# Hybrid GLA/mLSTM decoder layer on one core: token blocks stored by pieces, another place for a weight sum, down sums and gate rows on other queues and stages

## The chip, the cores and the metric

The kernel runs on 1 core of one Trainium2 chip. The metric is the device time in microseconds; the kernel before has a median of 1929.68 us over 3 runs (1927.24 to 1930.09). A core has five instruction streams that each run in order: TensorE (PE; its weight loads are shown as PEld), VectorE (DVE), ScalarE (ACT), GpSimd (POOL) and SyncE (SP). SP, ACT and POOL issue DMAs, which 16 DMA engines carry out.

## The reference, cut

One decoder layer in float32 over 16 meta tokens and 1024 tokens (1040 positions, width 1024):

```
h = concat([meta, x])                                    # 1040 x 1024
proj = rms_norm(h, norm_mix) @ w_in + b_in
g_q, g_k, g_v, g_r, g_lr, m_q, m_k, m_v, m_o, m_i, m_f, gate_a, gate_b = split(proj)
o_gla = head_rms(gla_chunked(...)) * silu(g_r)           # 4 heads, 128 keys, 256 values
o_ml  = head_rms(mlstm_chunked(...)) * sigmoid(m_o)      # 4 heads
y = sigmoid(gate_a) * (o_gla @ w_branch_gla) + sigmoid(gate_b) * (o_ml @ w_branch_ml)
h = h + y @ w_out
u = causal_dwconv(rms_norm(h, norm_ffn) @ w_up); gate, up = split(u)   # 2 x 2816
h = h + (silu(gate) * up) @ w_down
return rms_norm(h, norm_final)[16:]
```

## The kernel before

Every float32 product is made of three products of rounded halves: an operand is split into a high part (ScalarE copies and rounds it) and a low part (VectorE subtracts). So each weight tile goes through a DMA into a raw tile, a ScalarE split and a VectorE split before TensorE can use it. TensorE is kept full; the other engines and the queues run beside it.

**Order.** The program is written in Python generators, and a scheduler lays the instructions of each engine out in one list, by priority (`hp(n)` raises it) and by when it reckons that an instruction is ready. On the chip each list runs strictly in order. `issue_after(x)` keeps an instruction from being placed ahead of `x`. Tiles of one tag share `bufs` buffers; a new tile waits until the old one's readers are done.

**Stages**, by the profile:

1. Norm of x into `xH`, `xL` (to about 60 us).
2. Heads (to about 642 us): four GLA heads (s = 0 to 3), then four mLSTM heads (4 to 7). The main line makes projections; `main()` calls `advance()` 1.15 times per projection group, and each call moves one step of the current head's side work (`gla`, `mlstm`, `small_rows`) and one step of the closing work of an earlier head (`post`). A `yield` is the border of a step. `decay(s + 1)` is computed inside `gla(s)`. What is left when the projections are used up is run by `while side or closing: advance()`.
   In `post` of heads 3 to 6, `token_sums(k)` makes on POOL four sums and differences of token blocks for the products of the gate stage and stores them to the DRAM tile `tsc`; and `half_load`/`half_sums` load a part of `ffn_w_down` (on POOL), make four differences on POOL and store them to `tdn` (a down sum; 22 of them over the kernel: three in the heads, seven in the gate stage, six beside the first branch product, six beside the second). The first three gate rows of gate_b are projected at the end of the heads through the tile tagged "gst", which has one buffer.
3. Gate stage (to about 945 us): the gates g_r, m_o, gate_a and the rest of gate_b, two columns blocks at a time (13 pairs), by a Strassen-like scheme of seven block products (V, X, Y, Z banks in `piece`; the evacuations are at lines 997 to 1013). It needs the token blocks T1 to T4, which `token_blocks` loads from `tsc` in two pieces of 258 and 256 columns and `token_splits` splits; and sums of weight blocks, made in `gate_weights`, which `place` puts into one of four places: three buffers of the tags "wH"/"wL", and one of "w4H"/"w4L". Two gate_b projections (`COVER`) run on TensorE while the blocks are loaded. After each pair from the ninth on, down sums are made.
4. Branch products: o_gla @ w_branch_gla (`bg`, j = 0 to 7), then o_ml @ w_branch_ml (`bm`). `load_o` loads the gated head outputs on POOL. `sb` is the gate_b row j: loaded, put through a sigmoid on ScalarE, multiplied by the product on VectorE (L1257), added to `yg` (L1258) and split into `yH`, `yL` for the next product. Rows alternate between two single buffers ("hn" and "gst"). The `yg` rows lie in the tags Y0 to Y7.
5. Output product with w_out (`po`), whose results are added to the rows of x (`hacc`, tile h1 in Y0, h2 in Y1 and so on).
6. FFN up (to about 1685 us) and down, which the change does not touch.

Of the kernel before, what the change touches and what calls it, by code (L numbers as in the profile page):

```python
# [9 lines left out]
F32 = mybir.dt.float32  # L10
# [35 lines left out]
def hybrid_kernel(ctx, tc, x, meta, norm_mix, w_in, b_in, gla_w_gate, gla_b_gate, gla_norm,  # L46
# [407 lines left out]
            st[:, t0:t0 + n], p, AF.Copy), bank)  # L454
        nc.scalar.dma_start(gsc["b"][j], st[:, :NP])

    tsc = dram.tile([4, 4, P, 514], F32, name="tsc")

    def token_sums(k):

        a, b = (hd.tile([P, T], F32, name=f"x{i}{k}", tag="r", bufs=2) for i in "ab")
        t = wp.tile([P, T], F32, name=f"tx{k}", tag="gst", bufs=1)
        for y, i in ((a, k), (b, k + 4)):
            nc.gpsimd.tensor_tensor(y[:, :NP], xH[:, i, T0:].bitcast(F32), xL[:, i, T0:].bitcast(F32), OP.add)
        first, second = slice(0, 514), slice(512, NP)
        t1, t2 = t[:, 0:514], t[:, 520:1034]
        for dst, x, y in ((t1, a[:, second], a[:, first]), (t2, b[:, second], t1),
                          (a[:, second], b[:, second], a[:, second]), (b[:, first], b[:, first], t2)):
            nc.gpsimd.tensor_tensor(dst, x, y, OP.subtract)
        for i, src in enumerate((t1, t2, a[:, second], b[:, first])):  # L470
            nc.sync.dma_start(tsc[i, k], src)


    NP2 = NJ // 2
# [87 lines left out]
    def post(s, o, om, sc, ncols):  # L562

        h = s % 4
        g = "g" if s < 4 else "m"
        for c in range(NC):
            nc.scalar.activation(o(c), o(c), AF.Copy, scale=sc[:, c + 1:c + 2])
        nc.scalar.activation(om, om, AF.Copy, scale=sc[:2, 0:1])
        for _ in range(3 if s != 3 else 5):
            yield  # L570
        for j in range(2):
            of = hd.tile([P, T], F32, name=f"of{s}_{j}", tag="r", bufs=2)
            for gi in range(2):
                tp = ps.tile([P, 4, P], F32, name=f"ot{s}_{j}_{gi}", tag="s", bufs=3)
                for i in range(4):
                    nc.tensor.transpose(tp[:, i, :], o(4 * gi + i)[:, j * P:(j + 1) * P], ident)
                a, b = 2 + 512 * gi, 2 + 512 * (gi + 1)
                nc.scalar.activation(of[:, a:b], tp.rearrange("p n w -> p (n w)"), AF.Copy, scale=ncols[j])
                if gi == 0:
                    yield  # L580
            tp = ps.tile([P, 4, P], F32, name=f"otm{s}_{j}", tag="s", bufs=3)
            nc.tensor.transpose(tp[:, 0, :2], om[:, j * P:(j + 1) * P], ident[:2, :2])
            nc.vector.tensor_scalar(of[:, 0:2], tp[:, 0, :2], ncols[j], None, OP.mult)
            nc.sync.dma_start(osc[g][2 * h + j], of[:, :NP])
            yield
        if 3 <= s < 7:
            token_sums(s - 3)
            if s < 6:
                for _ in range(2):
                    yield  # L590
                t = half_load(wp, "gst")
                for _ in range(3):
                    yield
                half_sums(*t)
# [24 lines left out]
    def gla(s):  # L619
# [144 lines left out]

        if s < 3:
            decay(s + 1)
        up = ps.tile([P, 2, DV], F32, name=f"u0{s}", tag="s", bufs=3)
        nc.tensor.matmul(up[:, 0, :], K0, vt[:NM, 0, :DV], start=True, stop=True)
        S = state(f"S{s}")
# [259 lines left out]
    def gate_weights(q):  # L1029
# [9 lines left out]
        def place(name):  # L1039
            nonlocal ngw  # L1040
            ngw += 1
            if ngw % 4 == 0:
                return [gs.tile([P, NK, P], F32R, name=f"g{p}{name}_{q}", tag="w4" + p) for p in "HL"]
            return [wp.tile([P, NK, P], F32R, name=f"g{p}{name}_{q}", tag="w" + p) for p in "HL"]

# [34 lines left out]
    def token_blocks():  # L1080
        for i in (0, 2, 1, 3):
            if i == 1:
                places()
            TB[i] = [gs.tile([P, 4, 514], F32R, name=f"T{p}{i}", tag=f"T{p}{i}") for p in "HL"]
        for c in (slice(0, W0), slice(W0, 514)):
            for i in (0, 2, 1, 3):
                nc.sync.dma_start(TB[i][1][:, :, c].bitcast(F32), tsc[i].rearrange("k p c -> p k c")[:, :, c])

    def token_splits(p):
        c = (slice(0, W0), slice(W0, 514))[p]  # L1090
# [46 lines left out]
    for q in range(NG):  # L1137
# [18 lines left out]
            next(g)  # L1156
            behind_ = g
        if q >= NK:
            for _ in range(2 if q < NK + 2 else 1):
                half_sums(*half_load(gs, "o0"))  # L1160
    next(behind_)
    for j in END:
# [58 lines left out]
    for j in range(NK):  # L1221
# [7 lines left out]
        if j == 1:  # L1229
            with tc.issue_after(opened.ins), tc.issue_after(loaded.ins):  # L1230
                om_, loaded = load_o("m", r1b, "R", nc.gpsimd)
        for i in ((), (), (5, 6, 7), (6, 7), (7,), (), (), ())[j]:
            half_sums(*half_load(r2, f"Y{i}"))

    yH = [r2.tile([P, NK, 2, 256], F32R, name=f"yH{i}", tag=f"OH{i}") for i in range(2)]
# [6 lines left out]
        return t[:, 2:NP].rearrange("p (h q w) -> p h q w", h=2, q=2)[:, :, i, :]  # L1242

    for j in range(NK):
        if j % 2:
            sb = r2.tile([P, T], F32, name=f"sb{j}", tag="hn", bufs=1)[:, :NP]
        else:
            sb = wp.tile([P, T], F32, name=f"sb{j}", tag="gst", bufs=1)[:, :NP]
        with tc.issue_after(loaded.ins):
            nc.gpsimd.dma_start(sb, gsc["b"][j])  # L1250
        with tc.issue_after(opened.ins):
            nc.scalar.activation(sb, sb, AF.Sigmoid, bias=cc(C_GB + j))
        pt = prod3(ubm[j], om_, j < 1, f"bm{j}")
# [10 lines left out]
                nc.scalar.activation(yh, z, AF.Copy)  # L1264
                nc.vector.tensor_tensor(yL[i][:, j], z, yh.bitcast(F32), OP.subtract)
        if half:
            half_sums(*half_load(r2, f"Y{j if j < 3 else 3 - j % 2}"))
    r1b_ctx.close()
    ps2_ctx.close()
    psF = ctx.enter_context(tc.tile_pool(name="psF", bufs=1, space=PSUM, reuse_waits="tile"))  # L1270
# [7 lines left out]
    for t in range(NC + 1):  # L1278
# [1 line left out]
        if t == 0:  # L1280
            nc.sync.dma_start(a[:2, :D], meta[T0:NM, :])
        else:
            (nc.gpsimd if t in (3, 4, 7, 8) else nc.sync).dma_start(a[:, :D], x[P * (t - 1):P * t, :])
        hacc.append(a)
    gffn = wp.tile([P, T], F32, name="gffn", tag="gst", bufs=1)[:, :D]
    nc.sync.dma_start(gffn, rowb(norm_ffn, 0, D))
# [542 lines left out]
```

## Time and profile before

| | |
|---|---|
| runs | 1927.24, 1929.68, 1930.09 us |
| profiled execution | 1930.77 us, its span 1928.9 us |
| mean granted TensorE clock | 0.987 |
| TensorE busy | 1872.7 us |
| VectorE, ScalarE, GpSimd busy | 1196.0, 854.5, 399.6 us |
| DMA | 270.02 MB, mean 140 GB/s |

Times are us from the start of the span. In a list of instructions the columns are start, duration (from the first to the last, where several are merged), engine, line, operation, tiles (out<-in), forms and count; the bracket at the end holds how long the engine stood idle before it and what ended that. A row of a list of waits reads: engine and line that waited, on which engine's instruction, total us, times, longest. A row of windows gives for a stretch the busy time of each engine, the granted clock (PEclk, 1.00 is full speed), the share of the DMA engines' time and the rate. A queue row (q0: POOL's DMAs, q1: SP's, q10: ScalarE's) gives packets, MB and share.

### The profile page before, as it was taken

What the parts mean: (1) busy time and instruction counts of PE and PEld (TensorE: products, weight loads), DVE (VectorE), ACT (ScalarE), POOL (GpSimd) and SP (SyncE); (2) the same over time, 40 slices, a digit from 0 to 9 for tenths busy, and PEclk for the clock granted to TensorE, in tenths of its full rate; (3) what the DMA queues carried; (4) which work ended last, traced back from release to release, by engine and by line L of the source; (5) the groups of instructions that cost most, each with busy time, mean ns of one, the idle gap of its engine ahead of it and who ended that gap; (6) DMA issues with size and microseconds to landing.
All of it is one profiled execution on the core that took longest, in us unless ns stands there. A gap on an engine that the chain in (4) does not pass through costs nothing. (4 is left out here: it accounts for less than half of the span.)

```text
span 1928.9 us, 32657 instructions
## 1 busy us (share of the span) xinstructions
PE 1872.7 (97%) x13377; PEld 1789.9 (93%) x13377; DVE 1196.0 (62%) x1775; ACT 854.5 (44%) x1369; POOL 399.6 (21%) x441
## 2 busy tenths in 40 slices
PE   8999999989999999999899989999999999999998
PEld 8899989989998899999899989999999999987776
DVE  6556646564652456665442335788878788786777
ACT  5354555535553433332432224544344343455573
POOL 3101101130442001125461520012222222200000
PEclk8999999999999999999999989999999999999999
DMA  5111021051433737675973653423333333288794
GB/s 166 34 36 58 15 66 50 21 156 58 121 88 99 197 97 163 158 171 168 299 267 107 197 169 114 138 77 110 117 116 109 110 110 119 91 295 321 274 377 161
DMA packets 222592, 270.02 MB, mean 140 GB/s; under 512 B 13486, under 2 KB 176832, under 8 KB 222443
## 3 DMA queue, kind: packets, MB, share of 16 engines
q1 hardware_dynamic: 201467, 198.89, 33.8%
q0 software_dynamic: 16832, 58.80, 9.5%
q10 hardware_dynamic: 4144, 10.26, 1.5%
q8 instruction: 105, 1.72, 0.4%
q14 instruction: 44, 0.36, 0.1%
HBM read 198.33 MB, written 69.57 MB: 139 GB/s over the span
## 5 line engine op out<-in xcount | busy, mean ns | idle before, releaser
L489 POOL TENSOR_TENSOR ts<-ts 128x256 f32<-128x256 f32 x88 | 77.4, 884 | 64.9 <-DMA ts<-in_ffn_w_down_dram 62.6
L1389 POOL TENSOR_TENSOR SB<-SA,rg 128x512 f32<-128x512 f32 x20 | 32.1, 1607 | 236.0 <-issue 114.1
L1476 PE MATMUL po<-wH_wo,yH 128*128 128x256 f32 x256 | 74.2, 290 | 5.8 <-ACT wH_wo L106 4.9
L201 PE MATMUL pv<-wH_gv,xH 128*128 128x256 f32 x256 | 75.3, 294 | 0.0
L201 PE MATMUL pv<-wH_mv,xH 128*128 128x256 f32 x256 | 74.7, 292 | 0.1
L1476 PE MATMUL po<-wL_wo,yH 128*128 128x256 f32 x256 | 73.2, 287 | 0.9 <-DVE wL_wo L107 0.9
L1476 PE MATMUL po<-wH_wo,yL 128*128 128x256 f32 x256 | 72.9, 286 | 0.0
L201 PE MATMUL pv<-wH_gv,xL 128*128 128x256 f32 x256 | 72.0, 281 | 0.0
L201 PE MATMUL pv<-wL_gv,xH 128*128 128x256 f32 x256 | 72.0, 281 | 0.0
L201 PE MATMUL pv<-wL_mv,xH 128*128 128x256 f32 x256 | 72.0, 281 | 0.0
L201 PE MATMUL pv<-wH_mv,xL 128*128 128x256 f32 x256 | 71.9, 281 | 0.0
L1203 PE MATMUL bg<-ogH,wH_bg 128*128 128x342 f32 x192 | 62.3, 325 | 3.9 <-ACT ogH L1186 3.9
L1424 DVE SCALAR_TENSOR_TENSOR cv<-u,fc,cv 128x1024 f32<-128x1024 f32 x44 | 65.3, 1484 | 0.4
L699 POOL TENSOR_TENSOR pk<-pk,kT 128x256 f32<-128x256 f32 (+1 forms) x24 | 29.6, 1233 | 163.6 <-ACT pk L697 163.6
L1371 POOL TENSOR_TENSOR A<-u2raw,A 128x512 fp32r<-128x512 f32 x20 | 43.9, 2196 | 92.8 <-ACT A L1370 92.8
L1203 PE MATMUL bg<-ogL,wH_bg 128*128 128x342 f32 x192 | 62.1, 325 | 0.6 <-DVE ogL L1187 0.6
L1203 PE MATMUL bg<-ogH,wL_bg 128*128 128x342 f32 x192 | 61.9, 323 | 0.0
L1203 PE MATMUL bm<-omH,wH_bm 128*128 128x342 f32 x192 | 61.4, 320 | 0.0
L1203 PE MATMUL bm<-omH,wL_bm 128*128 128x342 f32 x192 | 61.3, 319 | 0.0
L1203 PE MATMUL bm<-omL,wH_bm 128*128 128x342 f32 x192 | 61.2, 319 | 0.0
L1476 PEld LDWEIGHTS po<-wH_wo,yH 128*128 128x128 f32 x256 | 49.3, 193 | 7.1 <-ACT wH_wo L106 5.1
L1713 POOL TENSOR_TENSOR fr<-fv,mhalf 128x1 f32<-128x1 f32 x8 | 6.4, 805 | 229.6 <-DVE fv L1711 229.6
(752 smaller groups left out, 7480.4 us busy)
## 6 DMA issues: line engine op xcount, KB each, us to landing
gw<-in_w_in_dram SPq DMA_DIRECT2D x26, 512.0 KB
ts<-in_ffn_w_down_dram POOLq DMA_DIRECT2D x44, 256.0 KB, 4.5
tdn<-ts POOLq DMA_DIRECT2D x44, 256.0 KB, 2.9
rg<-in_ffn_w_up_dram SPq DMA_DIRECT2D x22, 512.0 KB
ru<-in_ffn_w_up_dram SPq DMA_DIRECT2D x22, 512.0 KB
adr<-s SPq DMA_DIRECT2D x40, 256.0 KB
rd<-in_ffn_w_down_dram SPq DMA_DIRECT2D x20, 512.0 KB
do<-tdn SPq DMA_DIRECT2D x18, 512.0 KB
```

What stands on the lines that cost most here:

```text
L201: nc.tensor.matmul(pt[:, :DV], a[:, k, t0:t0 + P], b[:, k % 4, :], start=(i == 0), stop=(i == 3 * NK - 1))
L489: nc.gpsimd.tensor_tensor(t[:, o], t[:, a], t[:, b], OP.subtract)
L699: eng.tensor_tensor(e, e, k, OP.mult)
L1203: nc.tensor.matmul(pt[:, i, :n], a[:, k, :], b[k][:, t0:t0 + n], start=(k == 0 and j == 0), stop=(k == NK - 1 and j == 2))
L1371: eng.tensor_tensor(l, src, h.bitcast(F32), OP.subtract)
L1389: late.tensor_tensor(sb[:, 0:4], sa[:, 0:4], rg[:, 0:4], OP.subtract)
L1424: nc.vector.scalar_tensor_tensor(y, u[:, j:SEQ + j], fc[:, j, jj:jj + 1], y, OP.mult, OP.add)
L1476: nc.tensor.matmul(pt[:, :DV], a, b[:, k % 4, :], start=(k == 0 and i == 0), stop=(k == NK - 1 and i == len(terms) - 1))
L1713: nc.gpsimd.tensor_tensor(rs, v, mhalf, OP.pow)
```

## The change

- The token blocks are kept in DRAM as two tensors, one per piece, with a partition's four blocks of a piece side by side; `token_sums` stores each source in two pieces, from POOL instead of SP (32 stores instead of 16), and works in a tile of the tag "of" (two buffers) instead of "gst". `half_load` in `post` is kept behind the last of these stores.
- `post` of head 3 has six instead of five yields ahead of its transposes, and four more ahead of `token_sums`. `gla` has a yield after `decay`.
- `place` uses the fourth place for the third, seventh and so on instead of the fourth, eighth and so on.
- One down sum moves from after the last gate pair to j = 4 of the first branch product. The six beside the second branch product use Y0 and Y1 in turn.
- The gate_b rows of the second branch are loaded by SP instead of POOL and without the wait for the head outputs' loads; rows 6 and 7 lie in Y2 and Y3.
- Of the rows of x, tiles 1 and 2 are loaded by POOL and the others by SP; before, it was tiles 3, 4, 7 and 8 by POOL.

```diff
-    tsc = dram.tile([4, 4, P, 514], F32, name="tsc")
+    tsc = [dram.tile([4, P, 4, n], F32, name=f"tsc{n}") for n in (258, 256)]
...
-        t = wp.tile([P, T], F32, name=f"tx{k}", tag="gst", bufs=1)
+        t = hd.tile([P, T], F32, name=f"tx{k}", tag="of", bufs=2)
...
         for i, src in enumerate((t1, t2, a[:, second], b[:, first])):
-            nc.sync.dma_start(tsc[i, k], src)
+            for p in range(2):
+                stored = nc.gpsimd.dma_start(tsc[p][i, :, k], src[:, 258 * p:258 * p + 258 - 2 * p])
+        return stored
...
-        for _ in range(3 if s != 3 else 5):
+        for _ in range(3 if s != 3 else 6):
             yield
...
         if 3 <= s < 7:
-            token_sums(s - 3)
+            for _ in range(4 if s == 3 else 0):
+                yield
+            stored = token_sums(s - 3)
             if s < 6:
                 for _ in range(2):
                     yield
-                t = half_load(wp, "gst")
+                with tc.issue_after(stored.ins):
+                    t = half_load(wp, "gst")
...
         if s < 3:
             decay(s + 1)
+            yield
...
-            if ngw % 4 == 0:
+            if ngw % 4 == 3:
                 return [gs.tile([P, NK, P], F32R, name=f"g{p}{name}_{q}", tag="w4" + p) for p in "HL"]
...
-        for c in (slice(0, W0), slice(W0, 514)):
+        for p, c in enumerate((slice(0, W0), slice(W0, 514))):
             for i in (0, 2, 1, 3):
-                nc.sync.dma_start(TB[i][1][:, :, c].bitcast(F32), tsc[i].rearrange("k p c -> p k c")[:, :, c])
+                nc.sync.dma_start(TB[i][1][:, :, c].bitcast(F32), tsc[p][i])
...
         if q >= NK:
-            for _ in range(2 if q < NK + 2 else 1):
+            for _ in range((2, 2, 1, 1, 0)[q - NK]):
                 half_sums(*half_load(gs, "o0"))
...
-        for i in ((), (), (5, 6, 7), (6, 7), (7,), (), (), ())[j]:
+        for i in ((), (), (5, 6, 7), (6, 7), (6, 7), (), (), ())[j]:
             half_sums(*half_load(r2, f"Y{i}"))
...
-        if j % 2:
-            sb = r2.tile([P, T], F32, name=f"sb{j}", tag="hn", bufs=1)[:, :NP]
+        if j % 2 or j > 5:
+            sb = r2.tile([P, T], F32, name=f"sb{j}", tag="hn" if j < 6 else f"Y{j - 4}", bufs=1)[:, :NP]
         else:
             sb = wp.tile([P, T], F32, name=f"sb{j}", tag="gst", bufs=1)[:, :NP]
-        with tc.issue_after(loaded.ins):
-            nc.gpsimd.dma_start(sb, gsc["b"][j])
+        nc.sync.dma_start(sb, gsc["b"][j])
...
-            half_sums(*half_load(r2, f"Y{j if j < 3 else 3 - j % 2}"))
+            half_sums(*half_load(r2, f"Y{j % 2}"))
...
-            (nc.gpsimd if t in (3, 4, 7, 8) else nc.sync).dma_start(a[:, :D], x[P * (t - 1):P * t, :])
+            (nc.gpsimd if t in (1, 2) else nc.sync).dma_start(a[:, :D], x[P * (t - 1):P * t, :])
```

## The prediction

> **What bounds the kernel now.** I read the page's engine totals first, then TensorE's own list of waits, then the stretches around each wait, and last the instruction order of the other engines there.
>
> ```profile
> PE 1872.7 (97%) x13377; PEld 1789.9 (93%) x13377; DVE 1196.0 (62%) x1775; ACT 854.5 (44%) x1369; POOL 399.6 (21%) x441
> engine line waited for: us in total, times, longest us
> PE Xg L978 <- DVE gu L998: 5.7, 1, 5.7
> PE po L1476 <- ACT wH_wo L106: 4.9, 1, 4.9
> PE bg L1203 <- ACT ogH L1186: 3.9, 1, 3.9
> PE pv L188 <- ACT qT L438: 3.2, 1, 3.2
> PE op L911 <- DVE dn L914: 2.6, 2, 2.1
> PE ot L576 <- ACT of L578: 2.1, 1, 2.1
> PE u L768 <- DVE la L613: 2.1, 2, 1.0
> PE po L1476 <- DVE wL_wo L107: 0.9, 2, 0.7
> PE bg L1203 <- DVE ogL L1187: 0.6, 2, 0.3
> PE po L1476 <- ACT yH L1264: 0.5, 1, 0.5
> PE po L1476 <- DVE sb L1257: 0.4, 1, 0.4
> ```
>
> TensorE is busy 97% of the span, 1872.7 of 1928.9 us, and the change removes no matmul. It can only gain from the 56 us in which TensorE stands still, and from the lower clock that follows a stop:
>
> ```profile
> core 0: us, PE busy (x) PEld busy (x) DVE busy (x) ACT busy (x) POOL busy (x), PEclk, DMA share, GB/s
> 600.00:605.00 5.00, 3.81 (x11) 3.09 (x12) 1.77 (x6) 3.13 (x12) 0.00 (x0) 0.70 0.85 262
> 676.00:680.00 4.00, 3.73 (x17) 3.73 (x18) 0.54 (x2) 0.39 (x1) 0.00 (x0) 0.50 0.48 125
> 940.00:950.00 10.00, 5.79 (x34) 5.07 (x32) 2.55 (x3) 5.16 (x7) 4.28 (x9) 0.84 1.03 351
> 950.00:960.00 10.00, 9.77 (x50) 9.49 (x51) 6.58 (x6) 5.40 (x6) 3.21 (x7) 0.82 1.03 348
> 1140.00:1146.00 6.00, 4.46 (x16) 3.65 (x17) 4.99 (x8) 2.54 (x5) 0.53 (x1) 0.50 0.46 139
> 1146.00:1150.00 4.00, 4.00 (x28) 4.00 (x27) 3.30 (x8) 1.36 (x3) 0.53 (x1) 0.74 0.65 209
> ```
>
> The granted clock (PEclk) is 0.50 to 0.84 in these rows, which hold or follow the long waits. Busy time by (1 - clock) is what a stop costs on top: 3.81 x 0.30 = 1.1 us at 600; 3.73 x 0.50 = 1.9 at 676; 0.9 + 1.8 = 2.7 at 940 to 960; 2.2 + 1.0 = 3.2 at 1140 to 1150. Each part of the change touches one of these places.
>
> **Heads: the token sums and the yields.**
>
> ```profile
> 400.73 0.35 DVE L839 SCALAR_TENSOR_TENSOR wt<-MB,tcol,big 128x128 f32<-128x128 f32 x1
> 401.45 3.02 POOL L464 TENSOR_TENSOR xa<-xH,xL 128x1026 f32<-128x1026 f32 x1 [11.74 <-DMA oscg<-of]
> 404.62 8.11 DVE L839 SCALAR_TENSOR_TENSOR wt<-MB,tcol,big 128x128 f32<-128x128 f32 x6
> 412.81 1.28 ACT L841 ACT_TABLE_LOAD   x1 [11.50 <-DVE wt L839]
> 424.68 0.70 POOL L491 DMA_DIRECT2D tdn<-ts  x1
> 582.63 2.39 POOL L464 TENSOR_TENSOR xa<-xH,xL 128x1026 f32<-128x1026 f32 x1 [14.33 <-DMA oscm<-of]
> 599.84 0.46 ACT L453 ACTIVATE gb<-pj 128x342 f32<-128x342 f32 x1 [8.21 <-DMA tsc<-tx]
> 635.82 1.04 PE L576 MATMUL ot<-ident,or 128*128 128x128 f32 x8
> ```
>
> The first token sums start on POOL at 401.45, and one VectorE operation of L839 goes from 0.35 us to 8.11 / 6 = 1.35. ScalarE, in order, sits 11.50 us for their result, with TensorE's evacuations of qT queued behind it: that is the 3.2 us wait of L188. The change starts these sums one plus four yields later. A head has 15 projection groups, which at the pace of 1.15 make 17.25 steps; the first sums start at 401.45 and the fourth at 582.63, 60.4 us a head, so a step is 3.5 us and they start near 419, when L839 is done. They then slow other VectorE work; the smaller of the two L911 waits, 2.6 - 2.1 = 0.5 us, is the nearest price. I take -2.7 us (bounds -3.2 and 0).
>
> At 599.84 ScalarE has stood 8.21 us for the store of tx, because tx shares the one buffer "gst" with the row being evacuated; TensorE lost 2.1 us and 1.1 us of clock. In "of" there is no such sharing: -3.2 us (bounds -3.2, 0). The yield after decay puts projection matmuls between the pre-activation banks and the u product that waits 1.0 us for each of two: -2.1 (bounds -2.1, and 0 if the wait moves along). The sixth yield of head 3 lets its transposes come one group later than the 2.1 us wait of L576: half of it, -1.0 (bounds -2.1, 0).
>
> The 16 stores on SP become 32 on POOL. An issue there takes 0.70 us, so a head pays 5.6 us of an engine that is busy 21%; behind them stand the down load, its sums and the next head's root. On the path: 0 now; what it costs if POOL runs out is a rival below. SP loses 16 issues that waited for POOL in front of weight loads, also 0, since no weight wait of the heads is in the list. One cost: the side work was 68 yields of four GLA heads + 11 + 52 of four mLSTM heads + 7 of the last closing = 138, and the main loop gives 120 x 1.15 = 138 steps. Three more decay yields make 141, so the end of the last closing has no projection between it. Its 8 transposes took 1.04 us: +1 us (bounds 0 and 3 x 3.5 = 10). Heads together: -8.0 us.
>
> **Gate start: the token blocks by pieces and the third place.**
>
> ```profile
> 643.89 12.45 SPq L1087 DMA_DIRECT2D TL<-tsc  x8
> 668.02 1.06 ACT L1093 ACTIVATE TH<-TL 128x1024 fp32r<-128x1024 f32 x1 [3.26 <-DMA TL<-tsc]
> 672.52 0.39 ACT L997 ACTIVATE gu<-Vg 128x258 f32<-128x258 f32 x1 [0.40 <-ACT gb L453]
> 644.00:652.00 8.00, 8.00 (x53) 8.00 (x52) 2.66 (x4) 0.46 (x1) 0.00 (x0) 1.00 0.97 201
> q1 hardware_dynamic: 526, 0.92, 56.7%
> q0 software_dynamic: 513, 1.86, 98.5%
> ```
>
> Eight loads of some 0.52 MB (4.2 MB) take SP 12.45 us to issue and land until 668. ScalarE has the last split ahead of the first evacuation, which comes only at 672.52; X waits for it: the 5.7 us. The q1 row is 644 to 652: 0.92 MB in 526 packets, 1.7 KB each, with all queues at 201 GB/s. The q0 row is 945 to 950, the gate outputs in rows of 4.1 KB: 1.86 MB in 5 us, 372 GB/s. After the change a partition's block lies in one piece of 4128 or 4096 bytes, a quarter of the descriptors. At 372 GB/s the blocks are in by 644 + 11.3 = 656; at 201 GB/s by 665, still 3 us sooner, about the 3.26 us for which the last split waits. I take the first, since the row length is that of the q0 row. The third sum of pair 0 goes to the fourth place, free from the start, so its split need not wait for the cover products; what it displaces in later pairs is hidden, as the list has no other wait of the gate's own products. Gain 5.7 + 1.9 = 7.6 us (bounds 2 and 7.6).
>
> The Trainium skill (DMA: Bandwidth & Descriptors, "Why small descriptors are slow (HBM only)") speaks against this size: it puts the loss at about three cycles per packet beside its 32-byte beats, by my estimate 9% at 1032 bytes. By that the blocks come 1.6 us sooner, this term would be 2 instead of 7.6, and the time 1909; the 201 against 372 GB/s rows go beyond it, though other traffic is in both.
>
> **Gate end: six down sums.**
>
> ```profile
> 938.27 0.69 POOL L491 DMA_DIRECT2D tdn<-ts  x1 [0.30 <-POOL ts L489]
> 939.50 2.67 POOL L1185 DMA_DIRECT2D ogL<-otdg  x5
> ```
>
> POOL finishes the seventh sum at 938.27 and only then issues the loads that TensorE waits for. Without it POOL is free sooner by the course of one down sum, and 1 MB of traffic goes. The loads then wait for the gate's own tiles to come free. Stake 3.9 + 0.6 + 2.7 = 7.2 us. Against it: rows 0 and 1 of the second branch gate lose their wait on the loads and may go in here on SP, 1.05 MB at 351 GB/s, 3 us. I take -5 (bounds -7.2, 0). The sum itself moves to the first branch product, where TensorE has no row that waits for POOL: 0.
>
> **Second branch: gate rows on SyncE.**
>
> ```profile
> 1096.56 1.29 DVE L1265 TENSOR_TENSOR yL<-sb,yH 128x512 fp32r<-128x512 f32 x2 [0.36 <-ACT yH L1264]
> 1109.73 0.57 POOL L1250 DMA_DIRECT2D sb<-gscb  x1
> 1138.25 1.15 ACT L1252 ACTIVATE sb<-sb,col 128x1026 f32<-128x1026 f32 x1 [6.46 <-DMA sb<-gscb]
> 1139.31 1.04 ACT L106 ACTIVATE wH_wo<-wr_wo 128x1024 fp32r<-128x1024 f32 x1
> ```
>
> Row 5's buffer is free at 1097.8 but POOL issues its load at 1109.73, behind the down sums: 12 us lost. Rows 6 and 7 inherit it through the two buffers, and ScalarE's last sigmoid at 1138.25 stands ahead of the split of the first output weights. On SP row 5 goes at once, and rows 6 and 7 have own places (Y2, Y3) because the late sums keep to Y0 and Y1. A row on SP waits for the splits of the row two before; the weight load behind it is made two products ahead. Stake 4.9 + 0.7 + 0.5 + 0.4 + 3.2 = 9.7; I take -9 (bounds -9.7 and -4, a later row still in the way). The x rows swap queues; they are only added after the first output products: 0.
>
> **Sum.** -8.0 - 7.6 - 5 - 9 = -29.6. A list laid anew makes small waits; six of the present size of 0.5 us are +3. That is -26.6. The profiled execution took 1930.77 us (span 1928.9 and 1.87 around it), 1.09 over the median; off the median 1929.68 it leaves 1903.
>
> **Rivals.** (1) Half: SP becomes the crowded queue. Rows 0 and 1 delay the first branch's loads, rows 2 to 5 hold up weights behind them, and the heads trade waits. For: SP waits in nearly every stage. Against: no SP load's own lateness heads the list above. Gate start 5, branch edges 4 + 4, heads 2: 15, so 1915.
> (2) Slower: POOL cannot issue. Place: heads 3 to 6. A head has 60 us; sums and down sums take POOL from 401.45 to about 426, 25 us, and 8 stores come to them. From (60 - 25) / 8 = 4.4 us per store POOL sets the pace, and from 5.1 us it outweighs the 22 us gained elsewhere; at 6 us a head is 13 us longer, four heads 52, less 22: 1960. Against it: the row at 424.68 shows 0.70 us. For it: the L839 rows show that POOL and VectorE slow each other.
> That is also a rule of the Trainium skill (SBUF — State Buffer, "SBUF: two separate sides"): certain VectorE operations lock GpSimd out of a port it needs to write descriptors. The 0.70 us here is the issue with VectorE partly busy, so it has a small chance.
> (3) Nothing: every wait comes back one instruction later, since ScalarE and VectorE stay in order; 1928 to 1931.
>
> **How the numbers follow.** Forecast 0.60, its own range 1894 (all stakes: 35 us) to 1911; half 0.23, 1911 to 1925; slower 0.12; nothing 0.05. Within 0.2% (3.9 us) is what this measurement cannot tell from no change. Faster 0.83, same 0.05, slower 0.12. The range runs from 1894 to 1928 and leaves out mostly the slower case.
>
> **What would show it.** Right: no wait of X for gu over 1 us, the block splits done before the cover products end; the first bg product on the heels of the last gate product; no wait for wH_wo; no ScalarE wait for the tsc stores. Wrong: POOL issues over 2 us in the heads, SP waits for yL ahead of weight loads, or new TensorE waits above 3 us with a clock of 0.5 behind them.

## The result and the profile after

| | kernel before | changed kernel |
|---|---|---|
| device time, median (range), us | 1929.68 (1927.24 to 1931.8), 7 runs | 1923.57 (1917.53 to 1925.63), 7 runs |
| profiled execution, its span, us | 1930.77, 1928.9 | 1925.63, 1923.6 |

The ratio is 0.9964, 95% interval 0.9951 to 0.9976: faster by 6.1 us where 26.6 were forecast. Run once more in the experiments, beside the kernel before on one chip, the changed kernel took 1921.18 us to 1932.79, a ratio of 0.9936 (0.9923 to 0.9949). The gain is 6 to 12 us.

TensorE's list of waits in the changed kernel answers to the one shown of before; the rows left out are short, or as long as before (columns: microseconds in all, times, the longest):

```profile
PE Xg L984 <- DVE gu L1004: 9.2, 2, 8.1
PE bg L1209 <- ACT ogH L1192: 3.9, 1, 3.9
PE op L917 <- DVE om L902: 3.8, 2, 2.8
PE pdV L1630 <- DVE db L1610: 3.4, 2, 2.9
PE u L774 <- DVE la L618: 2.8, 3, 1.1
PE Yg L984 <- DVE gu L1012: 1.1, 1, 1.1
PE pe L158 <- ACT gu L1011: 1.0, 1, 1.0
PE ot L578 <- ACT of L580: 0.9, 1, 0.9
```

The waits for qT (3.2), for dn (2.6, now 0.8) and for wH_wo (4.9) are gone or small. The wait at the gate start has grown from 5.7 to 8.1, the one before the first branch product stands at 3.9 as before, and the waits for om are new.

Where the time went is read from the start of the same instruction in TensorE's timelines, in microseconds of the span; "again" is the second profile of the changed kernel, "all" the last experiment:

| first instruction of | before | changed | difference | again | all |
|---|---|---|---|---|---|
| cover product pc (end of the heads) | 641.95 | 639.13 | -2.8 | 638.67 | 632.35 |
| first S2 product, Xg<-TH,gHSB | 676.27 | 676.63 | +0.4 | 675.74 | 660.79 |
| first S4 product, Yg<-xH,gHSB | 685.35 | 685.18 | -0.2 | 685.70 | 667.89 |
| first branch product bg | 948.70 | 951.87 | +3.2 | 949.79 | 929.73 |
| second branch product bm | 1042.67 | 1045.06 | +2.4 | 1043.42 | 1023.17 |
| up product Vu | 1250.31 | 1242.35 | -8.0 | 1240.65 | 1220.42 |
| down product pdV | 1702.09 | 1693.74 | -8.4 | 1693.45 | 1672.36 |
| end of the span | 1928.9 | 1923.6 | -5.3 | 1919.7 | 1900.5 |

The gain is made between bm and Vu: 10.4 us, in both profiles of the changed kernel. The heads bring 3, and all or nearly all of it is lost before the first S2 product (+0.4 and -0.5 there). What differs between the two profiles of the changed kernel is no part of the change: the start-up (the first value product at 72.64 and 70.69, 71.31 before), the wait for db (3.4 and 1.2) and the small waits for gu at L1011 and L1012 (2.1 and 0.8), 5.5 us together. The two measured gains differ by as much, but half of that is the kernel before, which took 3.1 us longer on the second chip. Nor is a row of the table good to a microsecond: the run of the branch part alone, below, has the heads and the start of the gate stage unchanged, and there the first S2 product came at 677.96 after a wait of 7.2 us and bg at 952.52, where the column of before has 676.27, 5.7 and 948.70.

At the gate start VectorE's timeline shows what the S2 product waits for (columns: start, duration, instruction, and in brackets the idle time ahead of it and what ended it):

```profile
668.57 2.37 DVE L1100 TENSOR_TENSOR TL<-TL,TH 128x1024 fp32r<-128x1024 f32 x2 [4.09 <-ACT TH L1099]
672.23 0.69 DVE L1060 TENSOR_TENSOR gS<-gw,gw 128x512 f32<-128x512 f32 x1 [1.29 <-DMA gw<-in_w_in_dram]
672.96 0.69 DVE L1061 TENSOR_TENSOR gw<-gw 128x512 f32<-128x512 f32 x1
673.57 1.22 DVE L1043 TENSOR_TENSOR gLA<-gw,gHA 128x1024 fp32r<-128x1024 f32 x1
674.82 0.69 DVE L1066 TENSOR_TENSOR gw<-gw,gw 128x512 f32<-128x512 f32 x1
675.54 0.69 DVE L1067 TENSOR_TENSOR gw<-gw 128x512 f32<-128x512 f32 x1
676.15 0.42 DVE L1004 TENSOR_TENSOR gu<-Xg,gu 128x258 f32<-128x258 f32 x1
```

The add at 676.15 frees bank X. Five operations on the weights of the *next* pair stand ahead of it on VectorE's list, and the first of them waits for the load of those weights (gw), which SP issues behind the token blocks. Nothing of the present product is late. In the kernel before, ScalarE's split of the same weights and, from VectorE's list, the first and the last row behind it:

```profile
669.77 1.06 ACT L1036 ACTIVATE gHA<-gw 128x1024 fp32r<-128x1024 f32 x1 [0.35 <-DMA gw<-in_w_in_dram]
```

```profile
670.87 1.22 DVE L1037 TENSOR_TENSOR gLA<-gw,gHA 128x1024 fp32r<-128x1024 f32 x1 [0.53 <-ACT gHA L1036]
...
675.80 0.42 DVE L998 TENSOR_TENSOR gu<-Xg,gu 128x258 f32<-128x258 f32 x1
```

Six operations run there without a gap from 670.87 to the add: the same five, and gLSB, the split of the present pair's own third sum (1.22 us). The first of them waits, by way of ScalarE, for gw, which landed by 669.77; the last block's split had begun on ScalarE at 668.02, 1.8 us ahead of that.

SP's timeline, the stores of the last head and the issue of these loads, in the kernel before (its row of the block loads stands in the prediction) and in the changed one:

```profile
637.75 6.05 SPq L584 DMA_DIRECT2D oscm<-of  x2
656.39 31.76 SPq L1034 DMA_DIRECT2D gw<-in_w_in_dram  x4
```

```profile
638.48 1.82 SPq L586 DMA_DIRECT2D oscm<-of  x2
640.48 15.78 SPq L1093 DMA_DIRECT2D TL<-tsc  x8
656.37 31.61 SPq L1040 DMA_DIRECT2D gw<-in_w_in_dram  x4
```

TensorE reaches the cover product 2.8 us earlier, but SP issues the first of the stores 0.7 us later: in the kernel before it goes out 4.2 us ahead of the cover product, in the changed one 0.65 us. The block loads and gw stand behind it in SP's list, and gw goes out 18.6 us after the first store before and 17.9 us after it in the changed kernel, at the same time to 0.02 us.

At the gate end the timeline of GpSimd, then that of ScalarE:

```profile
931.73 2.09 POOL L1191 DMA_DIRECT2D ogL<-otdg  x4 [5.18 <-PE Xg L984]
937.84 2.09 POOL L1191 DMA_DIRECT2D ogL<-otdg  x4 [4.01 <-PE Zg L984]
```

```profile
947.91 1.06 ACT L106 ACTIVATE wH_bg<-wr_bg 128x1024 fp32r<-128x1024 f32 x1 [3.23 <-PE pe L158]
948.88 0.44 ACT L453 ACTIVATE gb<-pe 128x342 f32<-128x342 f32 x1
949.72 1.15 ACT L1231 ACTIVATE yg<-yg,col 128x1026 f32<-128x1026 f32 x1 [0.40 <-ACT gb L453]
950.77 2.94 ACT L1192 ACTIVATE ogH<-ogL 128x1026 fp32r<-128x1026 f32 x3
```

GpSimd issues the branch rows from 931.73 on, where before the first of them went out at 939.50, and TensorE still waits 3.9 us. The split at 950.77 shows no wait for a load. It follows three other things in ScalarE's list, the last a sigmoid that only an evacuation needs later.

### The profile page after: what moved, and what is told of

Read it like the earlier page. It is cut to its first block, busy times and chain, and to the rows that moved or that the text cites. A ratio compares the mean times of both kernels' runs of the same rounds, so it can differ in the third digit from the quotient of the medians.

```text
span 1923.6 us, 32692 instructions
## 1 busy us (share of the span) xinstructions
PE 1867.8 (97%) x13377; PEld 1785.1 (93%) x13377; DVE 1199.3 (62%) x1775; ACT 853.9 (44%) x1369; POOL 413.5 (21%) x463
## 5 line engine op out<-in xcount | busy, mean ns | idle before, releaser
L205 DVE TENSOR_TENSOR v<-pv,bB 128x256 f32<-128x256 f32 x64 | 26.8, 419 | 54.4 <-PE pv L201 54.3
```

The costliest lines, as they stand in the source:

```text
L205: nc.vector.tensor_tensor(vt[:n, c, :DV], pt[:n, :DV], bB[:n, :], OP.add)
```

## The experiments

The diffs are cut to the edit; line numbers shift by a few between kernels. Times beside them are medians, each with its ratio to the kernel before on the same chip.

### The token blocks in one run of memory

The store by pieces made the DRAM side of a block one run per partition, but the tile it lands in stayed [P, 4, 514], so that a piece is four runs there.

```diff
-TB[i] = [gs.tile([P, 4, 514], F32R, ...) for p in "HL"]
+TB[i] = [gs.tile([P, 4 * 514], F32R, ...) for p in "HL"]
...
-nc.sync.dma_start(TB[i][1][:, :, c].bitcast(F32), tsc[p][i])
+nc.sync.dma_start(flat(TB[i][1], p).bitcast(F32), tsc[p][i].rearrange("q k c -> q (k c)"))
```

> The changed kernel, with the SBUF side of each token block piece laid out in one run of 4128 or 4096 bytes as well. Run-length theory (the change left the packets at 1 KB because the SBUF tile is still cut into four runs a partition): TL packets become 4 KB, the eight issues on SyncE shrink below 8 us, the last block lands by 658 instead of 667, the wait of X for gu (8.1 us) falls under 2 us, time 1914 to 1917. Traffic theory (the slow stretch at 642 to 650 comes from what else is in flight, whatever the run length): packets are 4 KB, but the last block still lands after 664 and the wait stays above 6 us, time 1922 to 1925.

Measured: 1919.54, 0.9934 (0.992 to 0.9948), by its ratio no different from the changed kernel's second run. The DMA view of 644 to 652, queue and packets, megabytes, share of the engines' time, in the changed kernel:

```profile
q1 hardware_dynamic: 942, 1.16, 95.3%
```

in this one:

```profile
q1 hardware_dynamic: 322, 1.19, 96.8%
```

and in the changed kernel from 656 to 662:

```profile
q1 hardware_dynamic: 2084, 2.07, 107.9%
```

ScalarE's last split of the blocks here:

```profile
666.44 1.06 ACT L1101 ACTIVATE TH<-TL 128x1024 fp32r<-128x1024 f32 x1 [2.23 <-DMA TL<-tsc]
```

The packets are three times as long (3.7 KB against 1.2) and carry the same bytes in the same 8 us, some 0.15 MB a microsecond; in the third row packets of 1.0 KB carry 0.35. The last split starts at 666.44 instead of 668.6 (667.68 in the second profile of the changed kernel). gw is issued at 653.08 instead of 656.37, 3.3 us earlier, the wait of X for gu is 6.9 instead of 8.1 and 7.5, and the first S2 product starts at 674.4, 1 to 2 us earlier. That is little more than these profiles differ among themselves, but the earlier issue is clear of it. So the slow stretch that the prediction read from the window of 644 to 652 is not made by short packets.

### The second piece's splits behind the first evacuation

```diff
-    token_splits(1)
-weights_step(q + 1)
+    with tc.issue_after(evac[0].ins), tc.issue_after(evac[1].ins):
+        token_splits(1)
+        weights_step(q + 1)
```

> The changed kernel, with ScalarE's and VectorE's splits of the second token piece and of the next pair's first weights kept behind the first evacuation. List-order theory (the wait of X for gu comes from the evacuation's place in the two in-order lists, not from when the blocks land): X waits under 1 us though the last block lands as late as before, near 667; time 1914 to 1917. Landing theory (late blocks stop TensorE in any case): the wait moves to the first product that reads a second-piece block, Yg near 675, and is at least 5 us there; time 1921 to 1925.

Measured: 1923.68, 0.9952 (0.9936 to 0.9969); the wait is 9.1 us. VectorE's timeline:

```profile
676.85 0.69 DVE L1062 TENSOR_TENSOR gS<-gw,gw 128x512 f32<-128x512 f32 x1 [14.31 <-DMA gw<-in_w_in_dram]
677.58 0.69 DVE L1063 TENSOR_TENSOR gw<-gw 128x512 f32<-128x512 f32 x1
678.19 0.42 DVE L1006 TENSOR_TENSOR gu<-Xg,gu 128x258 f32<-128x258 f32 x1
```

The splits have gone from ahead of the add, and it is no earlier. The edit had missed two operations that a later step of the loop issues, and they alone hold the add until gw has landed. That excludes the blocks' splits as the cause and names the load of gw.

### Everything of the next pair behind the first evacuation

```diff
+def next_pair(q, f):
+    if q:
+        return f(q + 1)
+    with tc.issue_after(ev0[0].ins), tc.issue_after(ev0[1].ins):
+        f(1)
...
-                weights_step(q + 1)
+                next_pair(q, weights_step)
```

(in all three places; ev0 holds the first evacuation's two instructions, later the last split of the second piece)

> The changed kernel, with everything that VectorE and ScalarE do for the second token piece and for the next pair's weights held behind the first evacuation of the first gate product. List theory: TensorE's wait of 8.1 us before the first S2 product is not for the token blocks but for the first sums of the next pair's weights, which stand ahead of the add gu<-Xg,gu on VectorE's list and wait for a load of gw that lands at 672; with them behind it the add runs at about 665.5, the wait falls from 8.1 to under 1.5 us, and the time falls by about 6 us against the changed kernel, less what comes back as a new wait for the next pair's weights (up to 3 us). Landing theory of the prediction (the token blocks in memory decide): the wait stays at 7 us or more and the time is the changed kernel's, 1923.

Measured: 1913.48, 0.9899 (0.9884 to 0.9913). TensorE's waits, then VectorE's timeline:

```profile
PE Xg L984 <- DVE gu L1006: 0.5, 1, 0.5
```

```profile
665.85 0.43 DVE L1006 TENSOR_TENSOR gu<-Xg,gu 128x258 f32<-128x258 f32 x1 [4.89 <-PE Xg L984]
666.20 3.48 DVE L1102 TENSOR_TENSOR TL<-TL,TH 128x1024 fp32r<-128x1024 f32 x3
```

The add now waits for TensorE alone, the first S2 product starts at 668.47 instead of 676.63, and the S4 product 9.6 us earlier. The wait was one of order in VectorE's list.

### The same order in the kernel before

> The kernel before, with everything for the second token piece and for the next pair's weights held behind the first evacuation of the first gate product, and nothing of the change. List theory: TensorE's wait of 5.7 us before the first S2 product falls to 2 us or less although the third weight sum still lies in its old place and the blocks in their old layout, and the time falls by 4 to 8 us. Prediction's theory (layout and place decide): the wait stays at 5 us or more and the time is that of the kernel before.

Measured: 1924.14, 0.9949 (0.9936 to 0.9962). The first S2 product starts at 669.95 instead of 676.27 and no wait of X for gu is listed. With the old layout and the old place of the third sum the wait goes all the same, and this edit alone brings about as much as the whole change.

### The heads' part alone and the branch part alone

The first is the kernel before with the yields, the token sums' buffer and steps and the stores by pieces; the second, the kernel before with the gate rows on SyncE, their new places and the x rows' queues.

> The kernel before, with only the heads' part of the change: yields, token sums in the tag of, 32 piecewise stores on POOL, and the loads from the new layout. Theory that the heads gain some 5 us and the gate's first wait gives it back, because that wait ends with the blocks' landing and not with TensorE's arrival: time 1927 to 1931, the wait of X for gu 8 us or more. Rival, that the gain is kept: 1923 to 1925.

Measured: 1931.49, 0.9991 (0.9979 to 1.0002). The heads end at 639.12, the first S2 product starts at 677.41 after a wait of 8.3.

> The kernel before, with only the last part of the change: gate rows on SyncE, rows 6 and 7 in Y2 and Y3, the late sums in Y0 and Y1, the x rows' queues. Theory that this part alone holds more than the whole gain: the 4.9 us wait for wH_wo is gone, -9 to -10, time 1919 to 1921, lower than the changed kernel's 1923.6. Rival, that it needs the other parts: above 1923.

Measured: 1921.54, 0.9949 (0.9935 to 0.9963). The wait for wH_wo is gone. The product of the two ratios is 0.994, and the changed kernel's own, 0.9964 and 0.9936, lie on either side of it: the second branch is the change's gain, and nothing clear of the noise is left for the gate part, which was not run alone.

### The gate end: the sigmoid, and the seventh sum

```diff
-opened = nc.scalar.activation(y, y, AF.Sigmoid, bias=cc(C_GA + j))
+with tc.issue_after(ogsplit[0 if j else 7].ins):
+    opened = nc.scalar.activation(y, y, AF.Sigmoid, bias=cc(C_GA + j))
```

> The changed kernel, with the sigmoid of the first merge row behind the eight splits of the branch rows on ScalarE. List theory: TensorE's wait of 3.9 us before the first branch product is made of ScalarE's own list (last gate row, sigmoid, first split), the rows have long landed; without the sigmoid of 1.15 us ahead it falls to about 2.8 us, and the time by about 1 us. Load theory of the prediction (the rows' loads decide): 3.9 us stays, and so does the time.

Measured: 1921.1, 0.9935 (0.9921 to 0.9949). The wait is 2.8: it fell by the sigmoid. The time cannot tell 1 us.

The next kernel goes back to seven sums in the gate stage, `range(2 if q < NK + 2 else 1)` and `(7,)`.

> The changed kernel with seven down sums in the gate stage again, as before the change. Prediction's step (GpSimd's seventh sum holds back the loads that the first branch product waits for): the wait of 3.9 us grows to 5 us or more and the time by some 5 us, to 1929. List theory (ScalarE's list decides, the loads land in time with six sums and with seven): the wait stays between 3.5 and 5 us and the time within 2 us of the changed kernel's.

Measured: 1922.24, 0.9947 (0.9934 to 0.9959). TensorE's wait, then GpSimd's timeline:

```profile
PE bg L1209 <- ACT ogH L1192: 3.9, 1, 3.9
```

```profile
939.05 0.69 POOL L493 DMA_DIRECT2D tdn<-ts  x1 [0.30 <-POOL ts L491]
940.20 2.76 POOL L1191 DMA_DIRECT2D ogL<-otdg  x5
```

GpSimd is again late with the rows, by 8.5 us at the first of them, and the wait is the same to a tenth. The first row is not waited for, with six sums or with seven.

### The yield after the decay

```diff
         if s < 3:
             decay(s + 1)
-            yield
```

> The changed kernel without the yield after the decay in the heads. Prediction's step (the yield takes away waits of 2.1 us): the time is 2 us longer. Rival (the yield only moves these waits to the product u, three waits of 0.8 to 1.1 us for la): those three go, the old ones come back, and the time is within 1 us of the changed kernel's; what the heads gain or lose there is given back at the gate start anyhow.

Measured: 1914.67, 0.9909 (0.9893 to 0.9924), beyond what either theory gave. The heads end at 633.23, 5.9 us earlier, and the waits for om are gone. The last head's stores go out at 629.08, again 4.2 us ahead of the cover product, and the loads of the gate stage with them: gw is issued at 647.23, has landed by 663, and the first S2 product starts at 667.22. So this gain of the heads is not given back.

> The kernel before, with the yield after the decay of the heads and nothing else of the change. Theory that the yield itself costs (three heads close one step later, and the later heads' work falls together differently): the first cover product of the gate stage, 641.95 in the kernel before, comes 4 us later or more, and the time is 2 to 6 us longer, since TensorE's wait at the gate start absorbs part. Theory that it costs only together with the later token sums: the first cover product comes within 1.5 us of 641.95 and the time is within 2 us. Prediction's step: both come 2 us earlier.

Measured: 1928.89, 0.9975 (0.9965 to 0.9984), and the heads end at 634.83, 7.1 us earlier than before. None of the three expectations: alone the yield is a gain, larger than forecast, of which 3.4 us are left at the first S2 product. The last head's stores go out 0.66 us ahead of the cover product, at 634.17: 3.6 us earlier than in the kernel before where the heads end 7.1 us earlier, and gw and the S2 product follow the stores. The yield does not shorten the waits for la (2.1 before, 2.9 with it); it removes those for qT (3.2), most of dn (2.6 to 0.6) and head 3's wait for of (2.1), the very waits for which the prediction paid the later token sums, the tag "of" and the sixth yield. The rest of the heads' part removes them without the yield as well. The two do not add up, and together they bring the waits for om.

> The changed kernel without the four yields ahead of the first token sums; the yield after the decay and all else stay. Theory that the yield after the decay and the later sums are each a gain and together one step too many (the sums then run beside the convolution ahead of om on VectorE): the two waits for om of 3.7 us fall to about 1 us, the first cover product comes 3 to 5 us earlier than in the changed kernel (639), and the time is 3 to 6 us shorter. Theory that the yield alone is what brings the waits for om, wherever the sums stand: they stay at 3 us or more and the time is the changed kernel's. Prediction's step (later sums take away a wait of 3.2 us for qT): that wait comes back and the time is 3 us longer.

Measured: 1922.59, 0.9954 (0.9942 to 0.9966). The heads end at 638.97, the waits for om are 4.1. So the four added steps do nothing beside the yield, neither good nor bad, and the theory of one step too many is out. They do not even move the sums: the first starts at 408.79 here, at 409.69 and 407.62 in the two profiles of the changed kernel.

> The changed kernel with five yields instead of six in the closing of head 3; the yield after the decay, the later sums and all else stay. Prediction's step (the sixth yield takes 1.0 us off the wait for of): that wait grows by 1 us and the time with it. Theory of one step too many: everything behind head 3 stands one step earlier, the waits for om fall from 3.7 to 2 us or less, and the time is 2 to 5 us shorter.

Measured: 1925.9, 0.9971 (0.9961 to 0.9981). The waits for om stay (3.6) and the heads end at 643.28, 4.2 us later, where the other kernels with the heads of the changed one end them between 638.5 and 640.0. So the sixth yield is worth some 3 to 4 us there against the 1.0 us forecast; the ratio of the times, beside 0.9964 and 0.9936 of the changed kernel, does not settle it. Head 3's wait for of, which it was to shorten, is not there without it either; a new one of 1.5 us for vlo is, and what makes the rest of the 4.2 us is not shown.

### Two heads without the token sums

VectorE's list is the same in the changed kernel and here; only GpSimd's adds are left out in two heads, where unsummed rows are stored.

```diff
+if k in (1, 2):
+    for i in range(4):
+        for p in range(2):
+            c = T0 + 258 * p
+            stored = nc.gpsimd.dma_start(tsc[p][i, :, k], xH[:, k, c:c + 258 - 2 * p].bitcast(F32))
+    return stored
```

> The changed kernel, with the token sums of the second and third of the four heads that make them left out: GpSimd stores unsummed rows there, so these token blocks hold other values. VectorE's list in the heads is the same. Contention theory: the convolution rows ahead of om on VectorE (2.79 and 2.31 us, and 2.00, 1.94 in the changed kernel) are slow only because GpSimd adds beside them; without the sums they take 1.28 to 1.30 us, both waits for om (0.96 and 2.81 us) fall under 0.4 us, and the first cover product comes 3 to 4 us before 639. Order theory (the list puts om behind two more convolution rows): the waits stay at 2.5 us or more together.

Measured: 1917.45, 0.9939 (0.9923 to 0.9955). VectorE's timeline ahead of the first om that is waited for, and GpSimd's, in the changed kernel:

```profile
490.96 2.79 DVE L832 SCALAR_TENSOR_TENSOR kc<-kT,col,kc 128x1040 f32<-128x1040 f32 x1
493.67 2.31 DVE L832 SCALAR_TENSOR_TENSOR qc<-qT,col,qc 128x1040 f32<-128x1040 f32 x1
496.23 0.40 DVE L902 COPY om<-omp 2x257 f32<-2x257 f32 x1
```

```profile
490.24 2.40 POOL L464 TENSOR_TENSOR xb<-xH,xL 128x1026 f32<-128x1026 f32 x1 [3.02 <-ACT C L891]
492.72 2.16 POOL L469 TENSOR_TENSOR tx<-xb,tx 128x514 f32<-128x514 f32 x1
494.84 2.28 POOL L469 TENSOR_TENSOR xa<-xb,xa 128x514 f32<-128x514 f32 x1
```

and VectorE's without the sums:

```profile
492.27 1.29 DVE L838 SCALAR_TENSOR_TENSOR kc<-kT,col,kc 128x1040 f32<-128x1040 f32 x1
493.49 1.30 DVE L838 SCALAR_TENSOR_TENSOR qc<-qT,col,qc 128x1040 f32<-128x1040 f32 x1
495.16 0.41 DVE L908 COPY om<-omp 2x257 f32<-2x257 f32 x1
```

Without GpSimd beside them the two rows take 1.29 and 1.30 us, both waits for om are gone, and the heads end at 634.88, 4.25 us earlier; the first S2 product comes 4.4 us earlier too, at 672.2. The time's ratio cannot be told from the changed kernel's second one. The theory of contention holds. The times of the first two views also show how: kc starts at 490.96 and ends at 493.75, 1.1 us after xb has ended; tx then lasts until 494.88, 1.1 us after kc; qc until 495.98, 1.1 us after tx. They take turns, one whole instruction at a time. The Trainium skill (SBUF — State Buffer, "Who interferes with whom") states this: a VectorE operation with two inputs in SBUF and a GpSimd operation that reads SBUF exclude each other for a whole instruction. These rows agree.

### The changed kernel again, and all that was found together

> The changed kernel as it is, beside the other three, so that their times can be set against it on one chip. Expected by every theory: a ratio to the kernel before between 0.993 and 0.998, and the waits of its first profile (8 us before the first S2 product, 3.9 us before the first branch product, 3.7 us for om in the heads).

Measured: 1921.18, 0.9936 (0.9923 to 0.9949). The waits are 7.5 for gu, 3.9 for ogH and 3.7 for om.

The last kernel is the changed one with everything of the next pair behind the first evacuation, the sigmoid behind the splits, the blocks in one run of memory, and no yield after the decay.

> The changed kernel without the yield after the decay, with the evacuation first at the gate start, the sigmoid behind the branch rows' splits, and the token blocks in one run of memory on the SBUF side. If the three mechanisms found are separate they add up: the heads end about 6 us earlier, the wait before the first S2 product is under 1.5 us, that before the first branch product about 2.8 us, and the time is some 14 to 17 us under the changed kernel's, a ratio of about 0.988 to the kernel before. If the earlier heads only turn into a wait for the next pair's weights, it is the time of the run with the evacuation first less 1 to 2 us.

Measured: 1904.05 (1901.73 to 1906.46), 0.9848 (0.9832 to 0.9864): 28.7 us under the kernel before and 17.1 under the changed kernel, both on the same chip.

```profile
PE bg L1225 <- ACT ogH L1208: 2.8, 1, 2.8
PE u L773 <- DVE la L618: 2.1, 2, 1.0
PE bg L1225 <- DVE ogL L1209: 0.7, 1, 0.7
```

No wait of X for gu and none for om is left, and the mechanisms add up to the 17: the order some 10 us at the first S4 product (685.70 in the changed kernel's second profile, 675.6 with the order alone), the heads 6, the sigmoid 1.

## Why the prediction was wrong, by its own steps

**Heads, forecast -8.0, measured -2.8** (-4.1 and -2.7 in the two profiles when counted from the first value product). Four steps failed, and they are not independent.
- "The change starts these sums one plus four yields later ... and they start near 419, when L839 is done." They start at 409.69, and at 401.14 without the yield after the decay, where only the yields in `post` are left, against 401.45 before. What takes the wait for qT away in the changed kernel is ScalarE's list, in which qT's last evacuation now stands ahead of the instruction that waits for VectorE (before, that one came first, at 412.81):

```profile
410.03 0.53 ACT L438 ACTIVATE qT<-pj,col 128x346 f32<-128x346 f32 x1
419.21 1.28 ACT L847 ACT_TABLE_LOAD   x1 [5.91 <-DVE wt L845]
```

- "They then slow other VectorE work; the smaller of the two L911 waits ... is the nearest price." The mechanism was right and the size was not: 0.5 us was taken, and the run without the sums in two heads puts it at 3.8 us of waits, 4.25 us at the end of the heads. It falls due only beside the yield: without it no wait for om is listed. A row with such a price had been quoted: L839 at 1.35 us instead of 0.35 beside GpSimd's adds. As an estimate from it, 1.0 us a row makes 4 for the two convolution rows ahead of each of the two om; these grew by 1.5, 1.0, 0.7 and 0.65.
- The yield after the decay was to take 2.1 us off the waits for la. Those grew to 2.8; the bound named in the same sentence (the wait moves along) is what happened. Its real effect lay elsewhere, above all in the waits for qT and dn, which other terms had already been credited with. Terms that remove one wait by different parts were added up. Without the yield the heads end at 633.23, 8.7 us ahead of the kernel before, more than the other terms promised (-2.7 - 3.2 - 1.0); with it, 2.8. So this term, forecast at -2.1, is +5.9 in this kernel, and -7.1 alone.
- The sixth yield: -1.0 forecast, some -3 to -4 measured at the end of the heads. It did not work through the wait of L576, which is gone with five yields as well.

The wait for the store of tx is gone, as forecast. The slower rival needs 4.4 us per added store; the groups of GpSimd's instructions from 340 to 640 in the changed kernel refute it, with 0.58 each for 16 of the 32; the other 16 take 0.54 (the columns after the bar: busy time, mean ns of one, idle time ahead):

```profile
L472 POOL DMA_DIRECT2D tsc<-tx x16 | 9.3, 582 | 1.2 <-POOL tx L469 1.2
```

**Gate start, forecast -7.6, measured +3.2 from the end of the heads to the first S2 product.** The step that failed: "ScalarE has the last split ahead of the first evacuation, which comes only at 672.52; X waits for it." The row of the wait names VectorE's gu at L998, and the prediction read ScalarE's timeline. VectorE's would have shown the add at 675.80, 3.3 us later, behind the same five operations as in the changed kernel and gLSB. These begin when gw has landed, and gw is issued behind the token blocks on SP: 656.39 before, 656.37 after. So what the heads gained came back here as a longer wait, 8.1 instead of 5.7; the heads' part alone (0.9991) is that in pure form. The step behind it is a term of the heads: "so the end of the last closing has no projection between it" was priced at +1 for its transposes. What it cost is the 3.5 us by which the last head's stores fall back against the cover product in the kernels with the yield (0.65 and 0.66 us ahead of it, 4.2 without), because the block loads and gw stand behind these stores. In the kernels before and changed, in the one with the yield alone and in the changed one without it, the first S2 product starts 38.1 to 38.7 us after the first store. This is read from the profiles; no run moved the stores alone. The third sum's place took gLSB out of the way, 1.2 us, but gw landed later (670.49 against 669.77 on ScalarE), and it was no obstacle of its own (the wait goes without it). The quarter of the descriptors did not come about, since the tile kept the four runs; with them in one run, the last block came 1 to 2 us sooner. The rule of the Trainium skill that the prediction weighed (DMA: Bandwidth & Descriptors, "Why small descriptors are slow (HBM only)"), 1.6 us sooner by that estimate, was nearer than the 12 us taken from the window; the wait shrank by 0.6 to 1.2 us with them in one run, and went only with the order.

**Gate end, forecast -5, measured 0 on the wait.** The step that failed: "POOL ... only then issues the loads that TensorE waits for". The issue is earlier by 7.8 us, as forecast; it was not what the wait was made of. The wait is ScalarE's list from the last gate row to the first split, and falls by as much as is taken from this list. From the first S2 product to bg the changed kernel took 2.8 us longer in its first profile and 1.6 in its second. The branch part alone, which leaves this stage as it was but for two rows that SP loads at its end, took 2.1 us longer there, and the heads' part alone 2.0, so no edit to this stage can be shown to lose this time.

**Second branch, forecast -9, measured -10.4.** Right in mechanism and size: no wait for wH_wo, no wait on SP in its place.

**The allowance, forecast +3.** In the first profile the waits at L1011 and L1012 (2.1) and the growth of the one for db (1.3 to 3.4) are 4.2 us, in the second 0.8 with db at 1.2. The size is right only for the first, and that is luck, since these waits vary between two profiles of one kernel.

The first time measured, 1923.57, lies in the range of the first rival (half, 1911 to 1925), but by luck, not by its mechanism: no new wait leads to SP. The third rival's mechanism, a wait that comes back one instruction later because engines stay in order, is what held the gate start; it had been given the whole kernel or nothing, not one stage.

Not settled: why the yield brings the convolution rows beside GpSimd's sums in the changed kernel and hardly in the kernel before (1.1 us for om there), what makes the stretch of 644 to 652 slow, and why the eight block loads take 15.8 us to issue in the changed kernel and 12.5 before.

## What to carry to other kernels

When a wait names an engine and a line, read that engine's own timeline backwards from that line, not that of the engine that looks late; what stands ahead of it in its list, and what the first of these waits for, is the price. A gain upstream of a wait that ends at a landing is given back there unless the load goes out earlier by as much, as it did without the yield; so look for what stands ahead of the load in its queue's list, and count the gain from there. Terms that would remove the same wait by different edits are one term.

## What was not expected of the hardware

VectorE's operations with two inputs in SBUF and GpSimd's adds take turns by whole instructions, 1.3 us becoming 1.9 to 2.8 us on the one side and 1.3 becoming 2.2 on the other. A packet of 3.7 KB and one of 1.2 KB move at the same 145 to 149 GB/s in the slow stretch of 644 to 652, with the engines 95 to 97% busy, where the same queue moves some 345 GB/s (2.07 MB in 6 us) in packets of 1.0 KB ten microseconds later. And one interleaving step more or less, in three heads or in one, moved their end by 4 to 7 us, in either direction.
